# Embedding product ahead of the gate and kept in SBUF, rotary parts of a head over 128 partitions, splits behind scores and shares

## The chip, the cores and the metric

The kernel runs on one core of one Trainium2 chip. The metric is the device time of a run in microseconds (us). The kernel before took 1023.42, 1023.35 and 1022.2 us in three runs, median 1023.35. TensorE does the matmuls (PE in the rows; PEld is its weight load), VectorE is DVE, ScalarE is ACT, GpSimd is POOL; SyncE (SP) issues the transfers of weights.

## The reference

The reference is a trunk of two layers over 256 tokens of width 1024. Each layer is a half-step SwiGLU FFN, a token mixer, a second half-step FFN and a gated embedding; a last RMSNorm ends it. The mixer of the first layer is MLA, that of the second is FoX.

```python
for i in range(DEPTH):
    h = h + 0.5 * swiglu(rms_norm(h, ffn_norm[i, 0]), ffn_w_in[i, 0], ffn_w_out[i, 0])
    u = rms_norm(h, mix_norm[i])
    if i % N_MIXERS == 0:
        h = h + mla_mixer(u, cos, sin, w_down[j], q_norm[j], w_uq[j], kv_norm[j], w_ukv[j], w_o[j])
    else:
        h = h + fox_mixer(u, w_in[j], b_f[j], w_o[j])
    h = h + 0.5 * swiglu(rms_norm(h, ffn_norm[i, 1]), ffn_w_in[i, 1], ffn_w_out[i, 1])
    gate = jax.nn.sigmoid(rms_norm(h, ple_norm[i]) @ ple_w_gate[i])
    h = h + gate * (p[i] @ ple_w_proj[i])
return rms_norm(h, final_norm)
```

In MLA each of the 8 heads has a query of 128 plain and 64 rotary entries. A rotary pair is turned by the token's angle, `[x1*cos - x2*sin, x2*cos + x1*sin]`, and the rotary key is one for all heads. A score is `q_nope·k_nope + q_rope·k_rope`, times 192^-0.5, masked by chunks of 64 tokens. In FoX a score has a head dimension of 128 and a bias from a cumulative forget gate.

## The kernel before

The residual `hT` stays in SBUF, transposed: 8 blocks of 128 features by 256 tokens. All weights come from HBM as f32 blocks of mostly 128 x 1024 in the order of a list, `plan`. Products are taken in three terms to keep f32 precision: each weight is split into a high part `whi`, which ScalarE makes (L97), and a low part `wlo`, which VectorE makes (L101); the activations are split alike into a pair `u`. A block of products is then hi·hi, lo·hi and hi·lo (mm3, L213 to L215, three matmuls of 256 columns), or with both activation parts side by side one matmul of 512 and one of 256 columns (L228, L229).

The class `Weights` sets how far the splits run ahead. It holds 4 raw blocks and 7 pairs. `pump` splits one block: it gives ScalarE the next high parts, up to two ahead of the low ones, VectorE one low part, and SyncE the next transfer. Each call of `W.pump()` therefore puts about one whi and one wlo into the queues of ScalarE and VectorE at the place of the call. `get` takes a finished pair, `done` gives it back. The order of the instructions on each engine is the order in which the program issues them. PSUM has 7 banks that all products share in turn, named by their use (`ps`, `pe`, `psc`, `pt`, `po`), and one bank for small things.

RMSNorm is applied late. ScalarE squares each block, GpSimd adds the squares (`acc`, L288), four small matmuls sum over the partitions (`pst`, L302, `by_token`), VectorE scales the sum (`v`, L305), GpSimd takes the power of -0.5 (`rtok`, L307), four small matmuls turn it into a row for all partitions (`pb`, L312, `by_column`), and ScalarE copies it to `rb`. Products are multiplied by `rb` when they leave PSUM.

The embedding gate (`ple`, L757 to L840) goes through the 8 gate blocks d. Ahead of d = 0 and d = 4 it takes one block of the embedding's weight and makes four products into two `pe` banks, which stay in PSUM until they are used. Two gate blocks share a `ps` bank. `gated(d)` is the chain behind a block: VectorE zg = ps·rb (L763), ScalarE sg = sigmoid(zg) (L765), VectorE the low part of the block before, a pump, ge = pe·sg (L771), hT = hT + ge (L772), ScalarE the high part and the square for the next norm. In the last layer no low parts are made; there `hg` is transposed for the output.

In `mla` the query and key latents are normalised with `nq` and `nkv`. For a pair of heads `queries` makes the plain parts (copied by ScalarE) and the rotary parts: one bank with the rotary entries of both heads over 2 x 64 partitions and their swapped halves beside them. VectorE multiplies by cosine and sine (`tq`, L584) and GpSimd adds the two (L585). `kr` holds the turned key twice, in partitions 0 to 63 and 64 to 127, so that a score takes 64 rows of either half (L630).

`attention` is a software pipeline over heads: in step h it does the shares of head h-2 (`inv` and twice `pr`, L436 to L438, on VectorE), the products of head h, the output of head h-lag-1 (`po`, L451), the transposes of head h-lag (`pt`, L444, copied by ScalarE to `ptS`), and the scores of head h-1 (`psc`; VectorE takes the maxima `m` and the negative scaled maximum `nm`, ScalarE the two exponentials with their sums). Lag is 3 in MLA, 2 in FoX. A table (`MLA_FILLS`) says in which step how many matmul groups of the output projection are put between.

Of the kernel before, what the change touches and what calls it, by code (L numbers as in the profile page):

```python
# [25 lines left out]
H = 8  # L26
# [15 lines left out]

MLA_FILLS = {(8, 0): 4, (8, 1): 6, (9, 0): 5, (9, 1): 5, (10, 1): 4}
FOX_FILLS = {(8, 0): 4, (8, 1): 7, (9, 0): 6, (9, 1): 5}
# [96 lines left out]
def trunk(ctx, tc, xT, pT, pos, gains, freq, bf, ffn_first, ffn_in, ffn_out, w_down, w_uq, w_ukv, mla_o,  # L141
# [20 lines left out]
    def plan_ple(i):  # L162
        for d in range(KD):
            if d % 4 == 0:
                plan.append(ple_proj[i, d // 4])
            plan.append(ple_gate[i, d])

# [239 lines left out]
    def attention(project, score, v, scale, nxt, lag, fills, early, cumq=None):  # L407
# [91 lines left out]
        for h in range(H + lag):  # L499
            if 0 <= h - 2 < H:  # L500
                shares(h - 2)
            if h < H:
                project(h, 0)
            fill_some(fills.get((h, 0), 0))
            if 0 <= h - lag - 1:
                values(h - lag - 1)
            if 0 <= h - lag:
                turn(h - lag)
            if 0 <= h - 1 < H:
                scores(h - 1)  # L510
            if h < H:
                project(h, 1)
            W.catch_up()
            fill_some(fills.get((h, 1), 0))
            if h >= H:
                W.catch_up()
            ready = h - lag
# [14 lines left out]
    def keys_values():  # L532

        kqv = big.tile([P, 2 * KF, T], F32, name="kqv", tag="big")
        return kqv[:, :20, :], kqv[:, 20:28, :].rearrange("p (t c) n -> p t (c n)", t=2)


    def mla(norm, nxt):
# [5 lines left out]
        W.pump()  # L544
        block(pkv, norm.pair, norm.by_column)
        nq = Norm(G_Q, 2, 2 * P, tag="q")
# [22 lines left out]
        kq, v = keys_values()  # L569
        kT, qT, qr = kq[:, :8, :], kq[:, 8:16, :], kq[:, 16:20, :]  # L570
        held = []

        def queries(hp, half):
# [5 lines left out]
            if half == 0:  # L579
                nc.scalar.activation(qT[:, 2 * hp:2 * hp + 2, :], ps, AF.Copy)  # L580
            else:
                W.done(held[0])
                tq = work.tile([P, 2, T], F32, name="tq", tag="pair2", bufs=4)
                nc.vector.tensor_mul(tq, ps, cs)  # L584
                nc.gpsimd.tensor_add(qr[:, hp, :], tq[:, 0, :], tq[:, 1, :])  # L585
                W.pump()

        queries(0, 0)
        queries(0, 1)
        nkv.by_token()  # L590
        pk = bank("pk", (P, T))
# [4 lines left out]
        for hp in range(H // 2):  # L596
# [3 lines left out]
            pk.append(ps)  # L600
            if hp == 1:
                nq.by_token()
        W.done(w)
        nkv.by_column()
        for i in range(H // 2):
            nc.vector.tensor_mul(kT[:, 2 * i:2 * i + 2, :], pk[i], nkv.rb2)

        qscale = work.tile([P, 2], F32, name="qscale", bufs=1)
        nc.vector.tensor_scalar(qscale, nq.rtok, MLA_SCALE, None, op0=ALU.mult)
        w, = W.get()  # L610
        for t in range(2):
            for c in range(2):
                ps = bank("psv", (P, 512))
                mm3(ps, [nkv.pair[:, 0, a, t * P:(t + 1) * P] for a in range(2)],
                    [a[:, c * 512:(c + 1) * 512] for a in w[1:]], True, True)
                nc.scalar.activation(v[:, t, c * 512:(c + 1) * 512], ps, AF.Copy, scale=nkv.rtok[:, t:t + 1])
        W.done(w)
        W.pump(2)

        def project(h, half):  # L620
            if half == 0 and h < H - 2:
                queries(h // 2 + 1, h % 2)

        def score(h, dst, diagonal):
            r = slice(h % 2 * ROPE, (h % 2 + 1) * ROPE)
            for t in range(2):
                nc.tensor.matmul(dst[t], qT[:, h, t * P:(t + 1) * P], kT[:, h, :(t + 1) * P], start=t == 0, stop=False)
            masked(diagonal, 0)
            for t in range(2):
                nc.tensor.matmul(dst[t], qr[r, h // 2, t * P:(t + 1) * P], kr[r, :(t + 1) * P],  # L630
                                 start=False, stop=t == 1)

# [3 lines left out]
    def fox(norm, nxt):  # L636
# [80 lines left out]
        def project(h, half):  # L717
# [6 lines left out]
            (nc.vector if half else nc.gpsimd).tensor_add(kq[:, 2 * h + half, :], two[:, 0, :], two[:, 1, :])  # L724
            W.pump()

# [26 lines left out]
    def ple(pp, norm, nxt):  # L753
# [40 lines left out]
        po = ([], []) if nxt.gain is None else None  # L794
        waits = []
        for d in range(KD):
            if d % 4 == 0:
                w, = W.get()
                es = []
                for i in range(4):  # L800
                    if i % 2 == 0:
                        pe = bank("pe")
                    es.append(pe[:, i % 2, :])
                    part(es[i], w, pp, range(2), at=lambda k: k * 512 + i * P)
                W.done(w)
                if d:
                    W.pump()
            if d % 2 == 0:
                ps = bank("ps")
            block(ps[:, d % 2, :], norm.pair)  # L810
            waits.append((d, ps[:, d % 2, :], es[d % 4]))
            if d == 0:
                norm.by_token()
                W.pump(2)
            else:
                if d == 1:
                    norm.by_column()
                for x in waits:
                    gated(*x)
                waits = []  # L820
            if po and d >= 3:
# [192 lines left out]
def _layout(x, p, positions, ffn_norm, ffn_w_in, ffn_w_out, mix_norm, mla_w_down, mla_q_norm, mla_w_uq,  # L1014
# [29 lines left out]
    swap = np.concatenate([rope[..., 32:], rope[..., :32]], axis=-1)  # L1044
    w = np.concatenate([b.reshape(256, H // 2, -1) for b in (nope, rope, swap)], axis=-1)
    a["w_uq"] = _cols(w.reshape(256, -1), 512)
# [40 lines left out]
```

## Time and profile before

| what | before |
|---|---|
| runs, median | 1023.35 us |
| profiled execution | 1022.48 us |
| span in the profile | 1020.3 us |
| granted clock, mean | 0.993 |
| TensorE busy | 999.4 us, 98% |
| VectorE busy | 741.6 us, 73% |
| ScalarE busy | 516.7 us, 51% |
| GpSimd busy | 438.6 us, 43% |

The profiled execution took 1022.48 us, 2.2 us more than the span from its first to its last instruction. A busy share is an average: an engine at 98% still has 20 us in which it does nothing, and a low clock hides in the busy time. So the places in which TensorE waits are to be looked up in the timelines, where a row gives the idle time before an instruction and the instruction that ended it.

### The profile page before, as it was taken

What the parts mean: (1) busy time and instruction counts of PE and PEld (TensorE: products, weight loads), DVE (VectorE), ACT (ScalarE), POOL (GpSimd) and SP (SyncE); (2) the same over time, 40 slices, a digit from 0 to 9 for tenths busy, and PEclk for the clock granted to TensorE, in tenths of its full rate; (3) what the DMA queues carried; (4) which work ended last, traced back from release to release, by engine and by line L of the source; (5) the groups of instructions that cost most, each with busy time, mean ns of one, the idle gap of its engine ahead of it and who ended that gap; (6) DMA issues with size and microseconds to landing.
All of it is one profiled execution on the core that took longest, in us unless ns stands there. A gap on an engine that the chain in (4) does not pass through costs nothing.

```text
span 1020.3 us, 16281 instructions
## 1 busy us (share of the span) xinstructions
PE 999.4 (98%) x6050; PEld 884.4 (87%) x6050; DVE 741.6 (73%) x1057; ACT 516.7 (51%) x828; POOL 438.6 (43%) x364
## 2 busy tenths in 40 slices
PE   8999999999999999998999999999999999999987
PEld 6888888987988888888888888899889888888886
DVE  6777879676768787667777877666776778876663
ACT  6455444465555454445555444436545555444453
POOL 3677730221267765111277673120211577671121
PEclk9999999999999999999999999999999999999998
DMA  7566666541356665665556555665443576666531
GB/s 262 175 208 207 197 179 191 182 162 63 114 179 207 196 190 173 202 198 163 166 170 203 188 183 185 190 200 170 161 129 110 180 208 194 188 182 202 194 124 42
DMA packets 51534, 178.99 MB, mean 175 GB/s; under 512 B 6016, under 2 KB 6400, under 8 KB 51456
## 3 DMA queue, kind: packets, MB, share of 16 engines
q1 hardware_dynamic: 50736, 177.00, 55.1%
q10 hardware_dynamic: 720, 0.96, 0.3%
q8 instruction: 48, 0.79, 0.3%
q14 instruction: 30, 0.25, 0.1%
HBM read 176.89 MB, written 1.05 MB: 174 GB/s over the span
## 4 chain that ended last, share of the span: by engine, by line
PE 91%; DVE 4%; ACT 2%; issue 1%; DMA 1%; POOL 0%; SPq 0%; POOLq 0%; DVEq 0%; ACTq 0%
PE po L228 16%; PE pu L228 16%; PE pg L228 16%; PE po L229 8%; PE pu L229 8%; PE pg L229 8%; PE ps L228 4%; PE ps L229 2%; PE ps L213 2%; PE ps L215 2%; PE ps L214 2%; DVE wlo L101 1%; PE pv L213 1%; PE pv L215 1%; PE pv L214 1%
## 5 line engine op out<-in xcount | busy, mean ns | idle before, releaser
L101 DVE TENSOR_TENSOR wlo<-raw,whi 128x1024 fp32r<-128x1024 f32 (+2 forms) x338 | 417.7, 1243 | 8.1 <-ACT whi L97 7.9
L97 ACT ACTIVATE whi<-raw 128x1024 fp32r<-128x1024 f32 (+2 forms) x338 | 334.8, 1026 | 20.1 <-DMA raw<-in_ffn_in_dram 12.1
L328 POOL TENSOR_TENSOR gu<-two 128x256 f32<-128x256 f32 x176 | 235.6, 1340 | 119.5 <-DVE two L326 111.8
L228 PE MATMUL pg<-u,whi 128*128 128x512 f32 x704 | 252.0, 396 | 1.2 <-ACT whi L97 1.1
L228 PE MATMUL pu<-u,whi 128*128 128x512 f32 x704 | 251.4, 395 | 0.0
L228 PE MATMUL po<-hs,whi 128*128 128x512 f32 x704 | 246.3, 394 | 0.0
L229 PE MATMUL pg<-u,wlo 128*128 128x256 f32 x704 | 199.0, 283 | 0.6 <-DVE wlo L101 0.6
L229 PE MATMUL po<-hs,wlo 128*128 128x256 f32 x704 | 198.1, 281 | 0.0
L229 PE MATMUL pu<-u,wlo 128*128 128x256 f32 x704 | 198.1, 281 | 0.0
L228 PEld LDWEIGHTS pg<-u,whi 128*128 128x128 f32 x704 | 132.4, 188 | 32.5 <-ACT whi L97 1.7
L228 PEld LDWEIGHTS po<-hs,whi 128*128 128x128 f32 x704 | 132.2, 188 | 30.5
L228 PEld LDWEIGHTS pu<-u,whi 128*128 128x128 f32 x704 | 132.4, 188 | 29.9
L288 POOL TENSOR_TENSOR acc<-acc,sq 128x256 f32<-128x256 f32 x53 | 54.1, 1021 | 198.5 <-ACT sq L280 198.2
L229 PEld LDWEIGHTS pg<-u,wlo 128*128 128x128 f32 x704 | 132.6, 188 | 2.3 <-DVE wlo L101 1.7
L229 PEld LDWEIGHTS pu<-u,wlo 128*128 128x128 f32 x704 | 132.6, 188 | 0.0
L229 PEld LDWEIGHTS po<-hs,wlo 128*128 128x128 f32 x704 | 132.5, 188 | 0.0
L208 ACT ACTIVATE hs<-hid 128x256 fp32r<-128x256 f32 x88 | 36.8, 418 | 142.7 <-POOL hid L346 140.6
L346 POOL TENSOR_TENSOR hid<-sg,gu 128x256 f32<-128x256 f32 x88 | 104.2, 1184 | 6.9
L209 DVE TENSOR_TENSOR hs<-hid,hs 128x256 fp32r<-128x256 f32 x88 | 63.8, 725 | 47.6 <-ACT hs L208 47.6
L326 DVE TENSOR_TENSOR two<-pg,rb 128x512 f32<-128x512 f32 x88 | 60.3, 686 | 49.6 <-PE pg L229 40.8
L269 ACT ACTIVATE u<-hT,g_sb 128x256 fp32r<-128x256 f32 x57 | 29.0, 508 | 128.7 <-DVE hT L389 109.8
L340 ACT ACTIVATE sg<-gu 128x256 f32<-128x256 f32 x88 | 36.8, 418 | 80.6 <-POOL gu L328 80.6
(224 smaller groups left out, 1243.7 us busy)
## 6 DMA issues: line engine op xcount, KB each, us to landing
raw<-in_ffn_in_dram SPq DMA_DIRECT2D x172, 512.0 KB, 4.2
raw<-in_ffn_out_dram SPq DMA_DIRECT2D x64, 512.0 KB, 3.5
raw<-in_ffn_out_dram SPq DMA_DIRECT2D x32, 384.0 KB, 3.2
raw<-in_ple_gate_dram SPq DMA_DIRECT2D x16, 512.0 KB, 4.3
raw<-in_fox_qk_dram SPq DMA_DIRECT2D x16, 512.0 KB, 3.6
raw<-in_mla_o_dram SPq DMA_DIRECT2D x8, 512.0 KB, 4.3
raw<-in_fox_o_dram SPq DMA_DIRECT2D x8, 512.0 KB, 3.6
raw<-in_fox_v_dram SPq DMA_DIRECT2D x6, 512.0 KB, 4.5
```

Source lines behind the costliest of these rows:

```text
L97: self.nc.scalar.activation(self.pairs[i][0][:, c], self.raws[i][:, c], AF.Copy)
L101: self.nc.vector.tensor_sub(lo[:, c], self.raws[i][:, c], hi[:, c].bitcast(F32))
L208: nc.scalar.activation(hi, src, AF.Copy)
L209: nc.vector.tensor_sub(lo, src, hi.bitcast(F32))
L213: nc.tensor.matmul(ps, w[0], x[0], start=first, stop=False)
L228: nc.tensor.matmul(ps, hi, x[:, k], start=k == 0, stop=False)
L229: nc.tensor.matmul(ps[:, 1, :], lo, x[:, k, 0, :], start=False, stop=k == last)
L288: nc.gpsimd.tensor_add(new, self.acc, sq)
L326: nc.vector.tensor_mul(two, ps, norm.rb2)
L328: nc.gpsimd.tensor_add(gu[c, i], two[:, 0, :], two[:, 1, :])
L340: nc.scalar.activation(sg, gu.pop((c, 0)), AF.Silu)
L346: nc.gpsimd.tensor_mul(hid[c], gu.pop((c, 0)), gu.pop((c, 1)))
```

## The change

The two blocks of the embedding's weight move ahead of the gate's in the plan. Both products of the embedding are made at once, in four banks, and ScalarE copies each bank to a new tile `es` in SBUF. `by_token` comes after the first weight block, `by_column` in the middle of the second. Each gate block has a bank of its own and its `gated` follows at once. One pump less is called in the PLE.

In MLA the weight of the rotary parts is laid out so that one head's 64 rotary entries and their 64 swapped ones fill 128 partitions. One VectorE product by `ck`, which holds cosine in its upper and sine in its lower half, writes the result; the sum of both halves is left to the score's matmul, which now has 128 rows. GpSimd's additions go. `by_column` of the first norm moves behind the sixth instead of the fifth group, `nq.by_token` behind the first half of the values, pumps move behind `m` and `nm`, and the table of fills is spread over more steps (24 groups both). In FoX the last projection does not pump, and that pump comes behind the shares.

On TensorE, in the PLE of layer 0, gate block 3 followed block 2 in the same bank before (ps is the bank's tile, with its number):

```order
L213 MATMUL ps_5120<-u_3080,whi_4953 128x256
L214 MATMUL ps_5120<-u_3080,wlo_4954 128x256
L215 MATMUL ps_5120<-u_3080,whi_4953 128x256
L213 MATMUL ps_5120<-u_3080,whi_4979 128x256 [waits DVE_49,Activation_49]
L214 MATMUL ps_5120<-u_3080,wlo_4980 128x256
L215 MATMUL ps_5120<-u_3080,whi_4979 128x256
```

Now it has another:

```order
L211 MATMUL ps_5100<-u_3072,whi_4945 128x256
L212 MATMUL ps_5100<-u_3072,wlo_4946 128x256
L213 MATMUL ps_5100<-u_3072,whi_4945 128x256
L211 MATMUL ps_5144<-u_3072,whi_4971 128x256 [waits Activation_49]
L212 MATMUL ps_5144<-u_3072,wlo_4972 128x256 [waits DVE_49]
L213 MATMUL ps_5144<-u_3072,whi_4971 128x256
```

What moved: the first matmul of block 3 no longer needs VectorE to have read block 2; its second one waits for the low part of its own weight.

On TensorE, in the same PLE, the column statistic pb stood among gate blocks before:

```order
L213 MATMUL ps<-u,whi 128x256
L214 MATMUL ps<-u,wlo 128x256
L215 MATMUL ps<-u,whi 128x256
L312 MATMUL pb<-ident,rtok 128x128 [waits Pool_49]
L312 MATMUL pb<-ident,rtok 128x128
L213 MATMUL ps<-u,whi 128x256 [waits Activation_49]
```

Now it stands among the embedding's matmuls, twelve of them behind pst:

```order
L211 MATMUL pe<-q,whi 128x256
L212 MATMUL pe<-q,wlo 128x256
L213 MATMUL pe<-q,whi 128x256
L310 MATMUL pb<-ident,rtok 128x128 [waits Pool_49]
L310 MATMUL pb<-ident,rtok 128x128
L211 MATMUL pe<-q,whi 128x256
```

What moved: 24 matmuls stood between pst and pb, now 12 do.

On VectorE, in MLA's loop over heads, the first head's part read before:

```order
L584 TENSOR_TENSOR tq<-ps,cs 128x512
L101 TENSOR_TENSOR wlo<-raw,whi 128x1024
L416 TENSOR_REDUCE m<-psc 128x1
L417 TENSOR_REDUCE m<-psc 128x1
L420 SCALAR_TENSOR_TENSOR nm<-m,qscale 128x2
L436 RECIPROCAL inv<-den 128x2
L437 TENSOR_SCALAR pr<-pr,inv 128x128
L438 TENSOR_SCALAR pr<-pr,inv 128x256
```

and reads now:

```order
L583 TENSOR_TENSOR kqv<-ps,ck 128x512
L414 TENSOR_REDUCE m<-psc 128x1
L415 TENSOR_REDUCE m<-psc 128x1
L418 SCALAR_TENSOR_TENSOR nm<-m,qscale 128x2
L101 TENSOR_TENSOR wlo<-raw,whi 128x1024
L434 RECIPROCAL inv<-den 128x2
L435 TENSOR_SCALAR pr<-pr,inv 128x128
L436 TENSOR_SCALAR pr<-pr,inv 128x256
```

What moved: the split stands behind the maxima instead of ahead of them, and ahead of the reciprocal of the shares.

The diff, its core:

```diff
--- before.py
+++ after.py
@@ -40,7 +40,7 @@
 G_KV = 74
 
 
-MLA_FILLS = {(8, 0): 4, (8, 1): 6, (9, 0): 5, (9, 1): 5, (10, 1): 4}
+MLA_FILLS = {(6, 1): 3, (7, 1): 3, (8, 0): 3, (8, 1): 4, (9, 0): 4, (9, 1): 4, (10, 1): 3}
 FOX_FILLS = {(8, 0): 4, (8, 1): 7, (9, 0): 6, (9, 1): 5}
 
 PI_IN = 3.1415925
@@ -160,10 +160,8 @@
             plan.extend(ffn_out[i, d, :, a * P:min(a + KD, KF) * P] for a in range(0, KF, KD))
 
     def plan_ple(i):
-        for d in range(KD):
-            if d % 4 == 0:
-                plan.append(ple_proj[i, d // 4])
-            plan.append(ple_gate[i, d])
+        plan.extend(ple_proj[i, c] for c in range(2))
+        plan.extend(ple_gate[i, d] for d in range(KD))
 
     plan_ffn(0)
     plan.extend(w_down[c] for c in range(4))
@@ -501,6 +499,8 @@
                 shares(h - 2)
             if h < H:
                 project(h, 0)
+            elif h == H:
+                W.pump()
             fill_some(fills.get((h, 0), 0))
             if 0 <= h - lag - 1:
                 values(h - lag - 1)
@@ -532,7 +532,7 @@
     def keys_values():
 
         kqv = big.tile([P, 2 * KF, T], F32, name="kqv", tag="big")
-        return kqv[:, :20, :], kqv[:, 20:28, :].rearrange("p (t c) n -> p t (c n)", t=2)
+        return kqv[:, :24, :], kqv[:, 24:32, :].rearrange("p (t c) n -> p t (c n)", t=2)
 
 
     def mla(norm, nxt):
@@ -542,7 +542,7 @@
         blocks(pq, norm.pair)
         norm.by_token()
         W.pump()
-        block(pkv, norm.pair, norm.by_column)
+        block(pkv, norm.pair, norm.by_column, 6)
         nq = Norm(G_Q, 2, 2 * P, tag="q")
         nkv = Norm(G_KV, 1, P, tag="kv")
         cq = [tmp("cq") for _ in range(2)]
@@ -567,7 +567,7 @@
         W.pump()
 
         kq, v = keys_values()
-        kT, qT, qr = kq[:, :8, :], kq[:, 8:16, :], kq[:, 16:20, :]
+        kT, qT, qr = kq[:, :8, :], kq[:, 8:16, :], kq[:, 16:24, :]
         held = []
 
         def queries(hp, half):
@@ -580,13 +580,12 @@
                 nc.scalar.activation(qT[:, 2 * hp:2 * hp + 2, :], ps, AF.Copy)
             else:
                 W.done(held[0])
-                tq = work.tile([P, 2, T], F32, name="tq", tag="pair2", bufs=4)
-                nc.vector.tensor_mul(tq, ps, cs)
-                nc.gpsimd.tensor_add(qr[:, hp, :], tq[:, 0, :], tq[:, 1, :])
-                W.pump()
+                nc.vector.tensor_mul(qr[:, 2 * hp:2 * hp + 2, :], ps,
+                                     ck.rearrange("p (o t) -> p o t", o=1).to_broadcast([P, 2, T]))
 
         queries(0, 0)
         queries(0, 1)
+        W.pump()
         nkv.by_token()
         pk = bank("pk", (P, T))
         nc.tensor.matmul(pk, twice, turned, start=True, stop=True)
@@ -598,15 +597,10 @@
             for s in range(2):
                 part(ps[:, s, :], w, nkv.pair, range(1), at=lambda k: (2 * hp + s) * P)
             pk.append(ps)
-            if hp == 1:
-                nq.by_token()
         W.done(w)
         nkv.by_column()
         for i in range(H // 2):
             nc.vector.tensor_mul(kT[:, 2 * i:2 * i + 2, :], pk[i], nkv.rb2)
-
-        qscale = work.tile([P, 2], F32, name="qscale", bufs=1)
-        nc.vector.tensor_scalar(qscale, nq.rtok, MLA_SCALE, None, op0=ALU.mult)
         w, = W.get()
         for t in range(2):
             for c in range(2):
@@ -614,21 +608,27 @@
                 mm3(ps, [nkv.pair[:, 0, a, t * P:(t + 1) * P] for a in range(2)],
                     [a[:, c * 512:(c + 1) * 512] for a in w[1:]], True, True)
                 nc.scalar.activation(v[:, t, c * 512:(c + 1) * 512], ps, AF.Copy, scale=nkv.rtok[:, t:t + 1])
+            if t == 0:
+                nq.by_token()
+                W.pump()
         W.done(w)
-        W.pump(2)
+
+        qscale = work.tile([P, 2], F32, name="qscale", bufs=1)
+        nc.vector.tensor_scalar(qscale, nq.rtok, MLA_SCALE, None, op0=ALU.mult)
+        W.pump()
 
         def project(h, half):
             if half == 0 and h < H - 2:
                 queries(h // 2 + 1, h % 2)
+            elif half and h % 2:
+                W.pump()
 
         def score(h, dst, diagonal):
-            r = slice(h % 2 * ROPE, (h % 2 + 1) * ROPE)
             for t in range(2):
                 nc.tensor.matmul(dst[t], qT[:, h, t * P:(t + 1) * P], kT[:, h, :(t + 1) * P], start=t == 0, stop=False)
             masked(diagonal, 0)
             for t in range(2):
-                nc.tensor.matmul(dst[t], qr[r, h // 2, t * P:(t + 1) * P], kr[r, :(t + 1) * P],
-                                 start=False, stop=t == 1)
+                nc.tensor.matmul(dst[t], qr[:, h, t * P:(t + 1) * P], kr[:, :(t + 1) * P], start=False, stop=t == 1)
 
         attention(project, score, v, qscale, nxt, 3, MLA_FILLS, 4)
 
@@ -722,7 +722,8 @@
             two = work.tile([P, 2, T], F32, name="two", tag="pair2", bufs=4)
             nc.vector.tensor_mul(two, ps, norm.rb2)
             (nc.vector if half else nc.gpsimd).tensor_add(kq[:, 2 * h + half, :], two[:, 0, :], two[:, 1, :])
-            W.pump()
+            if (h, half) != (H - 1, 1):
+                W.pump()
 
         def score(h, dst, diagonal):
             for t in range(2):
@@ -792,32 +793,26 @@
 
         hgs = []
         po = ([], []) if nxt.gain is None else None
-        waits = []
+
+        es = big.tile([P, KD, T], F32, name="es", tag="big")
+        for c in range(2):
+            w, = W.get()
+            for i in range(4):
+                if i % 2 == 0:
+                    pe = bank("pe")
+                if (c, i) == (1, 2):
+                    norm.by_column()
+                part(pe[:, i % 2, :], w, pp, range(2), at=lambda k: k * 512 + i * P)
+                if i % 2:
+                    nc.scalar.activation(es[:, 4 * c + i - 1:4 * c + i + 1, :], pe, AF.Copy)
+            W.done(w)
+            if c == 0:
+                norm.by_token()
+            W.pump()
         for d in range(KD):
-            if d % 4 == 0:
-                w, = W.get()
-                es = []
-                for i in range(4):
-                    if i % 2 == 0:
-                        pe = bank("pe")
-                    es.append(pe[:, i % 2, :])
-                    part(es[i], w, pp, range(2), at=lambda k: k * 512 + i * P)
-                W.done(w)
-                if d:
-                    W.pump()
-            if d % 2 == 0:
-                ps = bank("ps")
-            block(ps[:, d % 2, :], norm.pair)
-            waits.append((d, ps[:, d % 2, :], es[d % 4]))
-            if d == 0:
-                norm.by_token()
-                W.pump(2)
-            else:
-                if d == 1:
-                    norm.by_column()
-                for x in waits:
-                    gated(*x)
-                waits = []
+            ps = bank("ps", (P, T))
+            block(ps, norm.pair)
+            gated(d, ps, es[:, d, :])
             if po and d >= 3:
                 by_token(d - 3)
         if po:
@@ -1042,7 +1037,8 @@
     w = mla_w_uq[0].reshape(256, H // 2, 2, 192)
     nope, rope = w[..., :128], w[..., 128:]
     swap = np.concatenate([rope[..., 32:], rope[..., :32]], axis=-1)
-    w = np.concatenate([b.reshape(256, H // 2, -1) for b in (nope, rope, swap)], axis=-1)
+    rope = np.concatenate([rope, swap], axis=-1)
+    w = np.concatenate([b.reshape(256, H // 2, -1) for b in (nope, rope)], axis=-1)
     a["w_uq"] = _cols(w.reshape(256, -1), 512)
     w = mla_w_ukv[0].reshape(P, H, 2, P)
     a["w_ukv"] = np.ascontiguousarray(w.transpose(2, 0, 1, 3)).reshape(2, P, D)
```

## Rows read from the trace of the kernel before

**Rows 1.** Page, parts 1 and 5: busy us, mean ns of one, idle before.

```profile
PE 999.4 (98%) x6050; PEld 884.4 (87%) x6050; DVE 741.6 (73%) x1057; ACT 516.7 (51%) x828; POOL 438.6 (43%) x364
...
L101 DVE TENSOR_TENSOR wlo<-raw,whi 128x1024 fp32r<-128x1024 f32 (+2 forms) x338 | 417.7, 1243 | 8.1 <-ACT whi L97 7.9
L97 ACT ACTIVATE whi<-raw 128x1024 fp32r<-128x1024 f32 (+2 forms) x338 | 334.8, 1026 | 20.1 <-DMA raw<-in_ffn_in_dram 12.1
...
L228 PE MATMUL pg<-u,whi 128*128 128x512 f32 x704 | 252.0, 396 | 1.2 <-ACT whi L97 1.1
```

**Rows 2.** Timeline of PE, PLE of layer 0 (start, us, ... [idle <-releaser]).

```profile
458.98 0.28 PE L213 MATMUL pe<-q,whi 128*128 128x256 f32 x1
...
464.70 0.50 PE L302 MATMUL pst<-ones,acc 128*128 128x1 f32 x4
...
467.98 0.61 PE L312 MATMUL pb<-ident,rtok 128*128 128x128 f32 x4
...
471.16 0.28 PE L215 MATMUL ps<-u,whi 128*128 128x256 f32 x1
475.13 0.55 PE L213 MATMUL ps<-u,whi 128*128 128x256 f32 x1 [3.69 <-DVE zg L763]
...
495.33 0.39 PE L228 MATMUL pg<-u,whi 128*128 128x512 f32 x1
```

**Rows 3.** Timeline of DVE, the same PLE.

```profile
460.89 1.77 DVE L101 TENSOR_TENSOR wlo<-raw,whi 128x1024 fp32r<-128x1024 f32 x1
...
471.58 0.42 DVE L763 TENSOR_TENSOR zg<-ps,rb 128x256 f32<-128x256 f32 x1
...
474.57 0.41 DVE L763 TENSOR_TENSOR zg<-ps,rb 128x256 f32<-128x256 f32 x1
...
475.63 1.77 DVE L101 TENSOR_TENSOR wlo<-raw,whi 128x1024 fp32r<-128x1024 f32 x1
...
477.76 0.42 DVE L772 TENSOR_TENSOR hT<-hT,ge 128x256 f32<-128x256 f32 x1
```

**Rows 4.** Timeline of POOL, the same PLE.

```profile
460.72 0.85 POOL L288 TENSOR_TENSOR acc<-acc,sq 128x256 f32<-128x256 f32 x1 [5.00 <-ACT sq L280]
465.48 1.62 POOL L307 TENSOR_TENSOR rtok<-v,mhalf 128x2 f32<-128x2 f32 x1 [3.91 <-DVE v L305]
...
475.58 0.73 POOL L288 TENSOR_TENSOR acc<-sq 128x256 f32<-128x256 f32 x1 [8.48 <-ACT sq L280]
```

**Rows 5.** Waits of PE in the PLE of layer 1 (us in total, times, longest).

```profile
PE ps L213 <- DVE zg L763: 3.6, 3, 3.0
```

**Rows 6.** A stretch of that PLE: busy us by engine, granted clock, DMA.

```profile
991.00:1002.00 11.00, 10.70 (x81) 10.46 (x81) 4.36 (x9) 3.76 (x9) 2.65 (x3) 0.89 0.01 1
```

**Rows 7.** Timeline of PE, MLA ahead of its loop over heads.

```profile
202.90 0.71 PE L312 MATMUL pb<-ident,rtok 128*128 128x128 f32 x4
...
213.37 0.58 PE L302 MATMUL pst<-ones,acc 128*128 128x1 f32 x4 [0.68 <-DVE v L305]
```

**Rows 8.** Timeline of PE, MLA's loop over heads.

```profile
222.28 0.92 PE L630 MATMUL psc<-kr,kqv 64*128 64x128 f32 x4
223.12 0.39 PE L213 MATMUL ps<-q,whi 128*128 128x256 f32 x1
...
239.66 0.82 PE L627 MATMUL psc<-kqv 128*128 128x128 f32 x4
240.32 0.27 PE L530 MATMUL psc<-cmask,identb 128*128 128x256 bf16 x1
...
242.41 0.70 PE L451 MATMUL po<-ptS,kqv 128*128 128x256 f32 x2 [0.98 <-ACT ptS L446]
```

**Rows 9.** Timeline of DVE, two late heads of that loop.

```profile
241.74 0.17 DVE L436 RECIPROCAL inv<-den 128x2 f32<-128x2 f32 x1 [1.25 <-ACT pr L430]
...
244.79 0.17 DVE L436 RECIPROCAL inv<-den 128x2 f32<-128x2 f32 x1 [1.25 <-ACT pr L430]
```

**Rows 10.** Timeline of PE, FoX, the last heads.

```profile
765.26 0.61 PE L444 MATMUL pt<-ident,pr 128*128 128x128 f32 x3 [0.81 <-DVE pr L437]
```

## The prediction

> **What bounds the kernel now.** I read the page first, then the list of who waits for whom on TensorE, then the timelines of TensorE, VectorE and GpSimd around each wait, last the table of stretches with the granted clock. TensorE is busy 98% of the span, and in the FFNs, which are most of it, it waited for a weight's high part for 1.1 us in all [rows 1]. The change adds no matmul and takes none away, so the only time to win is where TensorE stands still, runs at the lower clock, or pays more for a matmul than it must. There are four such places, and the change touches all of them: the two embedding gates ("PLE"), the MLA layer and the last head of the FoX layer.
>
> **Part 1, PLE of layer 0.** It lasts from the first embedding matmul at 458.98 to the first matmul of the next FFN at 495.33, 36.35 us [rows 2]. The nominal pace: 48 matmuls (24 of the embedding, 24 of gate block 0) take from 458.98 to 464.70, 0.119 us each; 24 matmuls and the statistics pair pst take from 464.70 to 467.98, so pst costs 3.28 − 24 × 0.119 = 0.42, and I price pb alike. 48 embedding and 192 gate matmuls plus the two small groups are 240 × 0.119 + 0.84 = 29.4 us. The missing 6.9 us are waits and slow clock: the largest, 3.69 us before 475.13, ends with VectorE's zg [rows 2], which released the bank. The reason is the shared bank: gate block 3 writes into the bank that block 2's zg reads, and that zg ran at 474.57, behind the splits and gates of blocks 0 to 2 [rows 3]. With a bank for each block TensorE no longer stops for it.
>
> What comes in its place is the column statistic pb. It now stands after 36 embedding matmuls and pst, not after 72 matmuls. pst runs at about 458.98 + 24 × 0.119 = 461.8 (its acc is ready at 460.72 + 0.85 = 461.6 [rows 4]) and ends at 462.3; the v that reads it is queued on VectorE behind a wlo that ends at 460.89 + 1.77 = 462.66 [rows 3]; then v and 1.62 us of rtok on GpSimd [rows 4] give 464.5, while TensorE arrives after 12 more matmuls, at 463.7. With the semaphores a new wait of 1.0 us. Queued behind it on TensorE is everything, so it counts in full. TensorE then ends its last gate block after 30.4 us: gain 5.9.
>
> VectorE cannot keep that pace for sure. When it was behind, one block took it 474.57 − 471.58 = 2.99 us without, and 477.76 + 0.34 − 474.57 = 3.53 us with a GpSimd addition beside it [rows 3, 4]; I take the first zg's 0.34 to its successor for the last term. TensorE needs 24 × 0.119 = 2.85 us a block. The loss is at most 0.7 us a block over the seven blocks, less what VectorE has in hand when block 1 begins and the 2.1 us that TensorE works on blocks 0 to 5 of the next FFN's input (6 × 768 columns at 0.119 us per 256) before it reads block 6's low part: between 0 (2.99 each time) and 2.7 us (3.53 each time), paid at the start of the next FFN. The split and the GpSimd addition become due within 0.05 us of each other (475.58 against 475.63 [rows 3, 4]), and ge, which used to read one operand from PSUM, now reads two from SBUF, so whichever of the two starts first, something on VectorE is late. I take 2.7, the nearest row. Net gain 3.2; between 2.0 (the stall also lowers the clock, below) and 5.9.
>
> The Trainium skill bears on this ("SBUF — State Buffer", section "SBUF: two separate sides"): a VectorE operation with two SBUF inputs and a GpSimd operation that reads SBUF take one shared port by an exclusive lock, the first holding it for its whole length. The row of the 1.77 us wlo beside the addition agrees. By that rule alone es in SBUF is a step back, and the sum is the one just taken; were es left out of the rule's reach, the term would be 5.9.
>
> The four copies of es per PLE lie on ScalarE, half idle over the span, ahead of nothing that TensorE waits for: cost 0. One pump fewer leaves the next FFN one weight less ahead; the cover is the stock of pairs there, and the 1.1 us of waiting in all [rows 1] shows no FFN near its end. If that cover were gone, it would be one split of 1.24 us [rows 1].
>
> **Part 2, PLE of layer 1.** The same waits: three for zg, 3.6 us in all, the longest 3.0 [rows 5], each some 0.16 longer from start to start (471.16 + 0.12 to 475.13 is 3.85 for 3.69 printed [rows 2]). In the stretch of 11 us that begins at the end of the longest the granted clock is 0.89 [rows 6], a part of it at the lower level, 1.2 GHz: 11 × 0.11 = 1.2 us. Sum 3.6 + 0.5 + 1.2 = 5.3, less the new wait at pb 1.0: gain 4.2 or 4.3, I take 4.2. Here no low part is made, so a block is shorter on VectorE and it keeps up; what follows the last block is untouched. Bounds 3.0 (clock not won) to 5.3 (no wait at pb).
>
> **Part 3, MLA.** The statistic pb comes before its rtok is quite ready (its four matmuls 0.71 us at 202.90 [rows 7] against 0.61 in the PLE [rows 2]). It moves behind three more matmuls: at most 3 × 0.119 = 0.36, I take 0.25. The statistic of the queries waits 0.68 for VectorE at 213.37 [rows 7], because v is queued behind tq and a split; moved behind half of the values it is ready long before: 0.7 with what it displaces. The two tq halves per head pair become one VectorE product into kqv, and 4 GpSimd additions go.
>
> The rotary matmuls: four with 64 rows took 0.84 us to the next start (222.28 to 223.12), four with 128 rows and the same columns 0.66 (239.66 to 240.32) [rows 8]. If 64 rows is the reason, 8 × 0.18 = 1.5 us of TensorE; the same time for both means 0. The Trainium skill ("TensorE: Matmul & The Clock Gate", section "LDWEIGHTS (loading the stationary operand)") says that the count of rows doesn't matter to a weight load; by it this term is 0, and the rows here speak against it only indirectly, since the 64-row matmuls also follow a bf16 one.
>
> In the loop over heads TensorE waits 0.98 at 242.41 for the copy of the shares [rows 8], which ScalarE does behind a whi. With the splits behind nm, inv and pr that chain begins 1.2 us earlier. But in the later heads VectorE and ScalarE are a closed chain: inv waits 1.25 for the exponentials in every head, with a period of 244.79 − 241.74 = 3.05 us [rows 9]. What TensorE saves there is waited away again. Of 1.5 + 1.0 = 2.5 I take about two thirds, 1.6, since five of the eight heads lie ahead of that stretch; bounds 0 and 2.5. MLA together 0.25 + 0.7 + 1.6 = 2.6, from 1.0 to 3.5. The number of splits in the loop is five before and after.
>
> **Part 4, FoX.** The transposes of the shares wait 0.81 at 765.26 [rows 10] for pr, queued behind a wlo. With the split behind pr the wait goes: 0.9, from 0.5 to 1.0.
>
> **Sum.** 3.2 + 4.2 + 2.6 + 0.9 = 10.9. The profiled execution took 1022.48, so 1011.6; the median of the runs stands 0.87 above it: **1012.5**.
>
> **Rivals.** A, GpSimd's additions fall beside nothing: part 1 gives 5.9, time 1009.8. For it the uncontended block of 2.99, against it the 0.05 us race. B, 128 rows cost what 64 did and the loop is bound by the VectorE and ScalarE chain: 1.6 lost, 1014.1. For it the 3.05 us period, against it the two rows of the pace. For the half of B that is in the rotary matmuls the rule of "TensorE: Matmul & The Clock Gate" in the Trainium skill speaks too; the other half of B is this kernel's own chain. C, the stall of 2.7 at the FFN's start lowers the clock as those of 3 us did: 1.2 lost, 1013.7. D, slower: the splits moved between the exponentials and the shares are exposed in the head loop. The five in the loop and the one just ahead of it are 6 pumps, each 1.03 us of whi and 1.24 of wlo [rows 1]; if the chain of a head has no slack where they now stand, 6 × 2.27 = 13.6 and the 1.6 of the loop are lost: 1012.5 + 15.2 = 1027.7. It decides once scores to transposes take more than the three heads of lag, 3 × 3.05 = 9.2 us [rows 9]; a split in that chain makes it 2.3 us longer at most, so this is unlikely. E, the change frees TensorE in the PLEs but the banks, held by ScalarE's copies of es behind whi, stop it as zg did: the 3.2 + 4.2 = 7.4 of both PLEs falls to about 0, 1019.9; with seven banks and four copies early in the PLE I doubt it.
>
> **How the numbers follow.** Forecast 0.40, A 0.20, B 0.16, C 0.08, D 0.05, E 0.05; 0.06 is left for several small misses together, half of them within 0.2% of before (about 2 us, what a measurement can tell). Range 1007.5 to 1017.5: it takes in forecast, A, B, C and the ends 1.0 and 3.5 of the MLA. Faster 0.91, same 0.04, slower 0.05.
>
> **What would show it.** In the PLEs no TensorE wait for zg; a wait of about 1 us at pb for rtok; a clock of 1.00 through both; ge at the end of layer 0's PLE late and a wait of 2 to 3 us on the low part in the first matmuls of the next FFN. In MLA no wait at pst, rotary groups of 0.66 us, GpSimd without additions. In FoX no wait at pt. I am wrong if TensorE still waits for banks in the PLE, if pb's wait is several us, or if the head loop grows beyond 27 us.

## The result, and the profile after

The changed kernel took 1010.08 us (median of 4 runs, 1009.76 to 1011.68) against 1022.98 us before: a ratio of 0.9876, 95% interval 0.9864 to 0.9888. Forecast were 1012.5 us, within 1007.5 to 1017.5. The profiled execution took 1010.07 us, its span 1008.1.

Stages from the starts of TensorE's matmuls in the two timelines, in us. "Loop" runs from the first score's matmul, "PLE 1" ends with its last gate matmul:

| stage | before | after | gain |
|---|---|---|---|
| MLA, first pkv matmul to first score | 20.61 | 19.95 | 0.66 |
| MLA, loop and rest, to the next FFN | 51.84 | 49.30 | 2.54 |
| PLE of layer 0 | 36.35 | 30.30 | 6.05 |
| FFN behind it | 185.57 | 188.18 | -2.61 |
| FoX, first to last score | 52.82 | 51.67 | 1.15 |
| PLE 1 | 35.76 | 31.08 | 4.68 |

They sum to 12.47, and the span became 12.28 shorter. The rest is at the two ends: MLA begins 0.19 earlier, and the program needs 4.37 instead of 4.09 us from its last computation to its end. The first lies ahead of all that was changed; why the end takes longer is not known. Over the ten traces of this case MLA begins between 199.83 and 201.05 us, and the end takes 4.08 to 5.00 us. All matmuls are the same in number, and the other stages stayed within 0.1 us. A stage repeats far better than a whole run: from the first score to the next FFN the five traces with the changed MLA took 49.30 to 49.34 us.

Who waits for whom on TensorE after the change, over the whole span (us in total, times, longest):

```profile
PE pg L226 <- DVE u L272: 2.3, 1, 2.3
PE pb L310 <- POOL rtok L305: 1.4, 3, 0.6
...
PE po L449 <- ACT ptS L444: 0.9, 1, 0.9
```

Before, the first such row was zg in six waits; it is gone:

```profile
PE ps L213 <- DVE zg L763: 8.5, 6, 3.7
```

In its place come the two waits that were forecast, pb for rtok and the FFN's pg for u. The same on TensorE's timeline:

```profile
461.17 0.71 PE L310 MATMUL pb<-ident,rtok 128*128 128x128 f32 x4 [0.61 <-POOL rtok L305]
...
490.60 0.50 PE L226 MATMUL pg<-u,whi 128*128 128x512 f32 x1 [2.35 <-DVE u L272]
...
972.78 0.49 PE L310 MATMUL pb<-ident,rtok 128*128 128x128 f32 x2 [0.62 <-POOL rtok L305]
```

From the start of the matmul ahead to these, less the usual 0.12, they cost 0.77, 2.51 and 0.78 us. A block of VectorE and GpSimd in the PLE of layer 0 shows where the second comes from. VectorE:

```profile
482.34 0.42 DVE L764 TENSOR_TENSOR zg<-ps,rb 128x256 f32<-128x256 f32 x1
483.01 0.48 DVE L272 SCALAR_TENSOR_TENSOR u<-hT,g_sb,u 128x256 fp32r<-128x256 f32 x1 [0.24 <-ACT u L267]
483.41 1.22 DVE L101 TENSOR_TENSOR wlo<-raw,whi 128x1024 fp32r<-128x1024 f32 x1
484.54 0.96 DVE L772 TENSOR_TENSOR ge<-es,sg 128x256 f32<-128x256 f32 x1
485.54 0.43 DVE L773 TENSOR_TENSOR hT<-hT,ge 128x256 f32<-128x256 f32 x1
485.88 0.42 DVE L764 TENSOR_TENSOR zg<-ps,rb 128x256 f32<-128x256 f32 x1
```

GpSimd beside it:

```profile
483.42 1.80 POOL L286 TENSOR_TENSOR acc<-acc,sq 128x256 f32<-128x256 f32 x1 [1.74 <-ACT sq L278]
```

The period is 485.88 - 482.34 = 3.54 us, against 2.85 us that TensorE needs for a block. The split has the start by 0.01 us and keeps its 1.22 us; the addition, 0.85 us long in [rows 4], is stretched to 1.80, and ge, which follows the split, takes 0.96 us instead of 0.42 and ends 0.28 us after the addition does (483.42 + 1.80 = 485.22). In three blocks it is so. In the two ahead of them the addition has the start, and it is the split that is stretched, with ge at its usual length; the period is the same but for the first of the two, 3.34 us:

```profile
476.32 1.77 DVE L101 TENSOR_TENSOR wlo<-raw,whi 128x1024 fp32r<-128x1024 f32 x1
478.01 0.41 DVE L772 TENSOR_TENSOR ge<-es,sg 128x256 f32<-128x256 f32 x1
```

```profile
476.27 0.73 POOL L286 TENSOR_TENSOR acc<-acc,sq 128x256 f32<-128x256 f32 x1 [2.81 <-ACT sq L278]
```

The rule of the Trainium skill ("SBUF — State Buffer", "SBUF: two separate sides"), that such a pair of operations takes the shared port in turn, agrees with these rows. In the first two blocks no addition falls beside VectorE's work, and it keeps TensorE's pace.

The granted clock (the number ahead of the DMA share and GB/s) is at its full level in both PLEs now, against 0.89 in [rows 6]:

```profile
465.00:486.00 21.00, 21.00 (x179) 21.00 (x179) 18.21 (x30) 13.06 (x24) 5.07 (x4) 1.00 0.44 136
486.00:496.00 10.00, 7.65 (x45) 6.46 (x44) 9.25 (x14) 6.46 (x11) 3.38 (x3) 1.00 0.32 103
967.00:998.00 31.00, 30.38 (x255) 30.13 (x255) 19.69 (x33) 18.17 (x34) 7.14 (x7) 1.00 0.19 69
```

In MLA's loop and in FoX, the rows that answer to [rows 8] and [rows 10]:

```profile
238.01 0.27 PE L530 MATMUL psc<-cmask,identb 128*128 128x256 bf16 x1
238.12 0.82 PE L631 MATMUL psc<-kr,kqv 128*128 128x128 f32 x4
238.59 0.58 PE L226 MATMUL ps<-os,whi 128*128 128x512 f32 x1
...
240.86 0.70 PE L449 MATMUL po<-ptS,kqv 128*128 128x256 f32 x2 [0.88 <-ACT ptS L444]
...
757.50 0.49 PE L442 MATMUL pt<-ident,pr 128*128 128x128 f32 x3
```

The rotary group takes 238.59 - 238.12 = 0.47 us instead of 0.84. The wait at po is still there with 0.88 us. FoX's transposes wait no more.

### The profile page after: what moved, and what is told of

The parts are those of the page before. It is cut to its first block, busy times and chain, and to the rows that moved or that the text cites. A ratio compares the mean times of both kernels' runs of the same rounds, so it can differ in the third digit from the quotient of the medians.

```text
span 1008.1 us, 16281 instructions
## 1 busy us (share of the span) xinstructions
PE 992.8 (98%) x6050; PEld 882.0 (87%) x6050; DVE 745.9 (74%) x1057; ACT 520.7 (52%) x836; POOL 435.8 (43%) x360
## 4 chain that ended last, share of the span: by engine, by line
PE 90%; DVE 5%; ACT 2%; issue 1%; DMA 1%; POOL 1%; SPq 0%; POOLq 0%; DVEq 0%; ACTq 0%
PE po L226 16%; PE pu L226 16%; PE pg L226 16%; PE po L227 8%; PE pu L227 8%; PE pg L227 8%; PE ps L226 4%; PE ps L227 2%; DVE wlo L101 2%; PE ps L213 1%; PE ps L211 1%; PE ps L212 1%; DVE u L272 1%; PE pv L211 1%; PE pv L213 1%
## 5 line engine op out<-in xcount | busy, mean ns | idle before, releaser
L226 PEld LDWEIGHTS po<-hs,whi 128*128 128x128 f32 x704 | 132.2, 188 | 30.4
L286 POOL TENSOR_TENSOR acc<-acc,sq 128x256 f32<-128x256 f32 x53 | 57.1, 1077 | 188.6 <-ACT sq L278 188.3
```

What stands on the lines that cost most here:

```text
L226: nc.tensor.matmul(ps, hi, x[:, k], start=k == 0, stop=False)
L286: nc.gpsimd.tensor_add(new, self.acc, sq)
```

## The experiments

The first four ran on one chip, the other four on another. Stages are read as in the table above. Five of the kernels (the first two, the late pb, the old fills, the old places) ran once; the four runs of the changed kernel lie 1.9 us apart, so what these five show is in their stages and not in their whole times.

**The PLE alone.** The kernel before with the hunks of the diff in `plan_ple` and `ple` (from `es` to `gated`), nothing of MLA and FoX.

> The kernel before with the PLE part of the change alone (plan, es, one bank per gate block, pb and pst among the embedding's matmuls, one pump less); MLA and FoX as before. Theory (the terms add, each is read in its own stage): PLE of layer 0 takes 30.3 us instead of 36.35, the FFN behind it 188.2 instead of 185.6, PLE of layer 1 31.1 instead of 35.8; the whole is 7.8 us shorter, 1014.7 against 1022.5 for the profiled execution of before. Rival (part of what the PLE seems to give comes from the weights' stock that MLA or FoX leave behind): the stages of the PLE differ from these by over 0.5 us, or the FFN behind waits for weights and not for u.

It took 1015.48 us, where 1014.7 had been expected. PLE 0 took 30.30, PLE 1 31.10, as in the changed kernel to 0.02; the FFN behind PLE 0 took 189.59, 1.4 more. The wait near its start is the same, 2.35 us for u, but not the clock after it. These are stretches of 5 us around the end of that wait, in this kernel and in the one with the late pb (further down):

```profile
493.00:498.00 5.00, 4.27 (x16) 3.70 (x17) 4.58 (x7) 3.60 (x7) 1.57 (x2) 0.66 0.22 90
```

```profile
488.00:493.00 5.00, 4.13 (x15) 3.56 (x16) 4.53 (x8) 3.59 (x7) 1.59 (x2) 0.68 0.22 89
```

In the changed kernel's profile it stayed at 1.00, and so it did behind the same wait in the kernels with the old fills and with the old places of the splits:

```profile
491.00:496.00 5.00, 4.40 (x25) 3.85 (x26) 4.70 (x7) 3.60 (x7) 1.58 (x2) 1.00 0.21 84
```

```profile
490.00:495.00 5.00, 4.05 (x23) 3.60 (x24) 4.53 (x8) 3.59 (x7) 1.59 (x2) 1.00 0.24 93
```

So the PLE's term stands by itself. Rival C (the stall at the FFN's start lowers the clock) came in two of the five profiles that have this wait, and cost 1.4 and 1.6 us of the FFN's stage there. The five are different kernels, but in this PLE and the FFN behind it four of them run the same program (this one, the changed kernel, the old fills, the old places), and the clock fell in one of the four. One of the changed kernel's four runs took 1011.68 us at a mean clock of 0.995, the others about 1010 at 0.997, which fits, but no trace of that run shows the place.

**128 rows alone.** The kernel before, whose scores then hold other numbers:

```diff
-            r = slice(h % 2 * ROPE, (h % 2 + 1) * ROPE)
+            r = slice(0, P)
```

> The kernel before, with nothing changed but the slice of the rotary score matmuls: 128 partitions instead of 64 (it adds the rotary products of both heads of a pair, so the scores are other numbers). Theory (64 rows are slower by themselves): from start to start the 128-column ones go from 0.163 to 0.110 us and the 256-column ones from 0.263 to 0.118, 3.1 us of TensorE less in 32 matmuls; MLA from its first pkv matmul to the next FFN gets 1 to 3 us shorter, the rest of the 3.1 being waited away in the later heads. Rival (64 rows only looked slow because they follow a bf16 matmul or another stationary size; the row count does not matter): the pace stays 0.16 and 0.26 us and MLA stays within 0.3 us of 72.45.

```profile
240.22 0.27 PE L530 MATMUL psc<-cmask,identb 128*128 128x256 bf16 x1
240.33 0.82 PE L630 MATMUL psc<-kr,kqv 128*128 128x128 f32 x4
```

It took 1022.22 us. The row count is the cause, but not in the way that the expectation has it: its 0.163 and 0.263 are middles between two different values. From start to start, the second 128-column matmul of a group and the first 256-column one take 0.112 and 0.218 us in both kernels. What differs lies at the ends of the group: from the mask's matmul to the first rotary one 0.20 instead of 0.11 us, from that to the next 0.21 instead of 0.11, from the last to the matmul behind the group 0.31 instead of 0.03, of which that matmul gives 0.08 back. So it is the change from 128 to 64 rows and back that costs, 0.39 us a head, 3.1 us of TensorE in eight.

But MLA's loop and rest took 51.13 instead of 51.84 us, 0.7 less (1 to 3 had been expected of MLA as a whole, which became as much shorter). Matmul by matmul, the first six heads bring nothing: the po behind them starts at 242.31 instead of 242.41, and the loop itself began 0.10 earlier. What they save is waited away ahead of pt and po, in pieces of up to 0.3 us and in two longer waits for ptS, 0.94 us at 238.47 and 1.17 at 242.31, where it was one of 0.98. The 0.7 us is what the last two heads save, behind the last of these waits.

**sg and ge in PSUM.** The changed kernel; each block has the free half of its bank for them.

```diff
-            zg, sg, ge = tmp("zg"), tmp("sg"), tmp("ge")
+            zg, sg, ge = tmp("zg"), z[1], z[1]
...
-            ps = bank("ps", (P, T))
-            block(ps, norm.pair)
-            gated(d, ps, es[:, d, :])
+            ps = bank("ps")
+            block(ps[:, 0, :], norm.pair)
+            gated(d, parts(ps), es[:, d, :])
```

> The changed kernel, with the sigmoid sg and the product ge written to the free half of the gate block's PSUM bank instead of to SBUF, so that ge and the addition to hT each read one operand from SBUF instead of two. Theory (ge with two SBUF operands stands still while GpSimd adds squares): ge falls from 0.94 to about 0.45 us, VectorE's period per block in the PLE of layer 0 from 3.54 to 3.0, and TensorE's wait of 2.51 us at the start of the next FFN falls below 0.6; the run is about 2 us shorter. Rival (VectorE simply has 3.5 us of work per block, or the split gets as much longer as ge gets shorter): period stays over 3.4, wait over 2.

VectorE and GpSimd in one block:

```profile
482.25 1.22 DVE L101 TENSOR_TENSOR wlo<-raw,whi 128x1024 fp32r<-128x1024 f32 x1
483.39 0.42 DVE L772 TENSOR_TENSOR ps<-es,ps 128x256 f32<-128x256 f32 x1
```

```profile
482.26 1.80 POOL L286 TENSOR_TENSOR acc<-acc,sq 128x256 f32<-128x256 f32 x1 [1.19 <-ACT sq L278]
```

With the addition running beside it just as before, ge takes 0.42 us. The period is 2.99 us in the blocks in which the split starts first, as expected, but still 3.34 and 3.54 in the two in which the addition does, and the wait at the FFN fell from 2.51 to 0.89 us (under 0.6 had been expected); the FFN stage went from 188.18 to 186.49. The run took 1009.63 us (1009.02 to 1009.76), a ratio to before of 0.9871, interval 0.9853 to 0.9889, where 2 us less than the changed kernel had been expected; it is not to be told from it. The last, halved block of PLE 1 lost 0.7 us, since the sigmoid of its first half then waits for both products zg and the first ge for both sigmoids; and in the profile the end of the program behind the last computation took 5.00 instead of 4.37 us.

**pb late.** The changed kernel:

```diff
-                if (c, i) == (1, 2):
-                    norm.by_column()
...
             if c == 0:
                 norm.by_token()
+            else:
+                norm.by_column()
```

> The changed kernel, with by_column behind all of the embedding's matmuls instead of in the middle of the second block. Theory (the wait at pb is only a matter of place): the two waits of 0.77 at pb go, the PLE of layer 1 gets 0.8 us shorter; in layer 0 the PLE gets 0.8 us shorter, and the wait at the start of the next FFN longer by what zg of block 0 comes later, under 0.3. Rival (VectorE's chain sets the end of layer 0 in any case): the wait of 2.51 at the next FFN grows by the whole 0.8 and layer 0 gains nothing.

PLE 0 took 29.42, PLE 1 30.21, each 0.87 us less; no wait at pb is left, and the wait at the FFN is 2.51 as in the changed kernel, not longer: the theory holds. The whole took 1009.04 us. The clock fell at the FFN's start (above), which took 1.6 us back, and MLA began 0.78 us earlier, which is no part of the edit.

**Old fills.** The changed kernel with the table of before:

```diff
-MLA_FILLS = {(6, 1): 3, (7, 1): 3, (8, 0): 3, (8, 1): 4, (9, 0): 4, (9, 1): 4, (10, 1): 3}
+MLA_FILLS = {(8, 0): 4, (8, 1): 6, (9, 0): 5, (9, 1): 5, (10, 1): 4}
```

> The changed kernel with the old table of fills in MLA. From MLA's first scores to the next FFN it took 51.84 us before, 51.13 with the rotary matmuls over 128 partitions alone and 49.30 in the changed kernel. Theory (what the changed kernel has beyond the faster matmuls comes from fills put into steps in which TensorE waits for the chain of scores and shares): with the old table this stretch goes back to 50.6 us or more, with new waits at po or pt in steps 6 and 7. Rival (the moved splits do it, the table does not matter): the stretch stays within 0.4 us of 49.3.

It took 1011.09 us. The stretch from the first score to the next FFN took 50.36: 1.06 us longer, a little under the 50.6 expected. The loop itself became 0.69 us shorter, since fills left it; what follows it became 1.75 longer. No new wait of size came; the one at po is 1.92 instead of 0.88:

```profile
240.93 0.70 PE L449 MATMUL po<-ptS,kqv 128*128 128x256 f32 x2 [1.92 <-ACT ptS L444]
```

**Old places of the splits.** The changed kernel:

```diff
                 queries(h // 2 + 1, h % 2)
-            elif half and h % 2:
-                W.pump()
+                if h % 2:
+                    W.pump()
...
-            elif h == H:
-                W.pump()
```

> The changed kernel with the splits in MLA's loop where they were, ahead of the maxima (behind the queries of the odd heads, none behind the scores, and none at the first step without a projection, in FoX neither). Theory (a split ahead of the maxima delays the chain that bounds the loop): the stretch from MLA's first scores to the next FFN gets 0.5 to 1.5 us longer than 49.3, with TensorE's waits at po longer. Rival (the fills cover it): within 0.4 us of 49.3.

It took 1010.33 us. The same stretch took 50.07, 0.77 us longer, with the wait at po a head earlier and about as long (0.94):

```profile
237.28 0.70 PE L449 MATMUL po<-ptS,kqv 128*128 128x256 f32 x2 [0.94 <-ACT ptS L444]
```

FoX stayed at 51.68 without the pump at the step behind the last projection: there the gain is that the split left its old place.

**Both improvements.** sg and ge in PSUM where it pays, in layer 0 (`if po` keeps the old tiles), and pb late in both.

> The changed kernel with sg and ge in the gate block's PSUM bank in layer 0 alone, and by_column behind all of the embedding's matmuls in both layers. Theory (both terms add; the loss of the first at the end of layer 1 comes only from the halved last block there): PLE of layer 0 29.4 us, the FFN behind it 186.5, PLE of layer 1 30.2 with the old tail of 9.7; 1010.1 - 0.85 - 1.7 - 0.85 = 1006.7. Rival (the FFN's wait for u grows by what the PLE is shorter, since VectorE's chain sets it): 1007.5 to 1008.

It took 1006.77 us (1006.67 to 1007.21), as expected (1006.7); ratio to before 0.9845, interval 0.9831 to 0.9858. PLE 0 29.42, FFN 186.51, PLE 1 30.21 with the old last block: both terms add as expected. The wait for u is 0.7 us, the only one on TensorE from the PLE's start to 40 us on:

```profile
PE pg L226 <- DVE u L272: 0.7, 1, 0.7
```

**And block 6's split behind the last block.**

```diff
-            if d < KD - 1:
+            if d < KD - 1 and (po or d != KD - 2):
                 W.pump()
...
                 nxt.last(d, src)
-                W.pump()
+                W.pump(2)
```

> The same, and in layer 0 the split of block 6 moved behind the last block (two there). Theory (the rest of the wait at the next FFN, 0.9 us, is one split of 1.2 us too many in VectorE's chain ahead of block 6's low part): the wait falls below 0.2 us and the run is 0.7 us shorter than the other, 1006.0. Rival (the sigmoid's time, until now hidden by that split, takes its place, or the FFN waits for its third weight instead): within 0.3 us of the other or longer.

It took 1006.45 us (1005.69 to 1006.73), ratio to before 0.9839, interval 0.9826 to 0.9853. No wait is left at the FFN, which took 185.64, 0.87 less than in the last one and as long as before the change. In the runs the difference is 0.3 us, where 0.7 had been expected, and the intervals overlap: this last step is seen in its stage and not in the whole time. In the two profiles the end of the program took 5.00 us here and 4.37 in the last one, which hides most of it.

## Why the prediction was right

- **PLE 0**: forecast 30.4 us for the stage, measured 30.30; lag 2.7, measured 2.51 of wait and 2.61 of stage; period 3.53, measured 3.54. The wait at pb was forecast as 1.0 and was 0.77. Net 3.2 against 3.44. The cause of the lag is shown by the third experiment, where ge does the same work with one operand less in SBUF (its result goes to PSUM too, which that run does not separate). That the lag's size came out is partly luck, for two of its parts were off and cancel. I let all seven blocks be late, 7 × 0.68 = 4.8 us, and took 2.1 us of TensorE's work off. The rows have five late blocks: the last zg, at 489.40, is 3.2 us behind TensorE's pace. And of the 2.1 us only 0.7 are left, since the low part that the FFN waits for stands behind the last block's zg on VectorE and is done 1.1 us after that zg's start, and the hand-overs between the engines take the other 0.3: 3.2 - 0.7 = 2.5.
- **PLE 1**: 4.2 against 4.68. The wait of pb was 0.2 less, and the low clock cost 1.4 instead of 1.2: the longest wait ended at 990.60, and the stretch of [rows 6] begins at 991.00.
- **FoX**: 0.9 against 1.15.
- **The weight less ahead**: cost 0, as argued. With its other waits gone the FFN behind PLE 0 took 185.64, before 185.57.
- **MLA**: 2.6 against 3.2, and here the single steps were not right. Ahead of the loop I forecast 0.25 + 0.7, and 0.66 came: the first pb gave 0.34 and the wait at pst went, but the second pb now waits for its rtok, 0.33 us longer from start to start. In the loop I sized the rotary term by comparing it with the plain group in [rows 8], 0.18 us a head; it was 0.39. I took two thirds of it and of the wait at 242.41, since five of the eight heads lie ahead of the closed chain; the rows say the opposite, in the second experiment those ahead of its last wait gave nothing, and the two behind it gave the 0.7 that was left of the 3.1. That wait stayed, with 0.88 for 0.98. And the fills, to which I gave no value of their own, were worth 1.06, the splits 0.77. The 2.54 of the loop is 0.7 + 0.77 + 1.06, and the runs lead there step by step: 51.84 us, 51.13 with 128 rows, 50.36 with the splits moved too (the run with the old fills), 49.30 with the fills; by the other way it is 50.07 with rows and fills. What fills and splits bring without the 128 rows was not run. So it is the chain of scores and shares, with what fills TensorE's waits for it, that set the time; that part of the argument, from [rows 9], held. That the loop came within 1 us of its 1.6 is in part luck, since the wait that was to go stayed and the fills were priced at nothing.
- **The rest of the 2.4 us** by which the forecast was too long: 0.87 that I added because the profiled execution of before was faster than the median. For the changed kernel both are the same, 1010.07 and 1010.08.

Of the rivals, A (additions beside nothing) is out by the rows of ge; B (128 rows cost the same) by the second experiment in its first half, while its second, that the loop gives little of it, was right for that term; C came in two of the five profiles with that wait, not in the changed kernel's. D and E did not come: splits behind the scores made the loop shorter, and no bank was waited for.

## What to carry to other kernels

Price a faster instruction by the chain of its stage: the matmuls with 128 rows saved 3.1 us of TensorE and, alone, 0.7 us of time, that of the heads behind the last wait. When an operand moves from PSUM to SBUF, look at what GpSimd does in the same microsecond. A wait that follows from an order may vanish when the waiting instruction moves behind work that needs nothing from it, as with pb, at no cost.

## What was not expected of the hardware

Weight loads for the 64-row matmuls take as long as those for 128 rows, a median of 187 against 192 ns; in this the Trainium skill ("TensorE: Matmul & The Clock Gate", "LDWEIGHTS (loading the stationary operand)") agrees. But ahead of the first load of each head's group the load engine stood 0.3 us with no release to wait for, 2.5 us in all, and as long again ahead of the load behind the group in six of the eight; within a group the pace was that of 128 rows. Kernel before, then the one with 128 rows, their weight loads (duration min/median/max):

```profile
L630 PEld LDWEIGHTS psc<-kr,kqv x32: 182/187/188, 222.3 to 248.9; 64*128 64x128 f32 x32
its engine sat idle before it (us, times) until:
  issue: 2.5, 8
```

```profile
L630 PEld LDWEIGHTS psc<-kr,kqv x32: 190/192/192, 222.0 to 248.3; 128*128 128x128 f32 x32
```

The first head's loads on the timeline, kernel before and then the one with 128 rows:

```profile
222.27 0.52 PEld L630 LDWEIGHTS psc<-kr,kqv 64*128 64x128 f32 x4 [0.32 <-issue]
223.12 0.19 PEld L213 LDWEIGHTS ps<-q,whi 128*128 128x128 f32 x1 [0.33 <-issue]
```

```profile
221.97 0.53 PEld L630 LDWEIGHTS psc<-kr,kqv 128*128 128x128 f32 x4
222.53 0.19 PEld L213 LDWEIGHTS ps<-q,whi 128*128 128x128 f32 x1
```

Why the change of rows is dear no run here shows. Nor is it settled why the same wait of 2.35 us was followed by the full clock in three profiles and by a stretch at 0.66 to 0.68 in two.
